# A hybrid encoder: splitting the mixer's weights ahead of the mixer and keeping the parts in DRAM

## The chip, the cores and the metric

One core of a Trainium2 chip runs the whole program. The metric is the device time of one execution in microseconds (us). Five engines take part: PE multiplies matrices (its weight loads are listed apart, as PEld), DVE and POOL work element by element on vectors, ACT evaluates functions and copies, and SP only issues DMAs. Each engine works through its own list of instructions in order; semaphores hold an instruction until what it needs is there.

## The reference

Two layers, on 512 tokens of width 1024, all in float32:

```python
for layer in range(DEPTH):            # DEPTH = 2
    x = x + 0.5 * swiglu(rms_norm(x, ffn1_norm), ffn1_w_in, ffn1_w_out)     # inner width 2816
    x = x + hybrid_mixer(rms_norm(x, mix_norm), w_in, ..., w_out, slopes)
    x = x + 0.5 * swiglu(rms_norm(x, ffn2_norm), ffn2_w_in, ffn2_w_out)

def hybrid_mixer(h, ...):
    aq, ak, av, bu, cq, ck, cv, dq, dk, dv = split(h @ w_in)    # 18 blocks of 128 columns
    o_a = windowed attention with a sink;  o_c = dilated attention;  o_d = neighbourhood attention
    y_b = s5_bidirectional(bu, ...); g = gelu(y_b); y_b = g * sigmoid(g @ w_glu)
    return concat(o_a, y_b, o_c, o_d) @ w_out
```

`s5_bidirectional` is a linear recurrence over the tokens in both directions.

## The kernel before

The activations `x` stay on the chip, transposed: 8 tiles of 128 features by 512 tokens. A product is made at float32 precision from three matmuls (`mm3`, lines 107 to 109): each operand is split into a high part, which is its rounding to the format fp32r, and a low part, the remainder; line 107 multiplies one low part, line 108 the other, line 109 the two high parts. So every weight goes through three steps. `load` (line 113) has SP fetch up to 128x1024 raw weights into a `wr` tile (ring of 2). Then, in pieces of at most 512 columns, line 125 has ACT cast a piece into `wh` (ring of 4), and line 126 subtracts: `wl = wr - wh` (ring of 4). Line 126 runs on DVE, or on POOL where `pooled=True`, which all weights of the mixer have but its first two blocks and `wg`.

`ffn` runs 22 passes over f in four groups. A pass takes two weight tiles of 1024 columns (gate and up), 48 matmuls of 512 columns, and a chain of DVE and ACT operations that writes `a`. After each group, eight products with `w2` (768 or 640 columns) add into `x`. In the first feed-forward of a layer `s5_tables` prepares tables for the recurrence: a Python generator (`hooks`) of which one step is taken per pass, at a lower priority.

`mixer` projects (`wm`, 18 blocks of 1024 columns), does the attentions and the recurrence (`s5`), and merges (`woD`, `woB`, `woC`, `woA`). A string, ORDER, sets the order in which the code calls these steps. In the recurrence DVE scans (lines 823, 825), then `zr` and `zi` are formed from products of DVE (832, 835) and POOL (833, 836, tile `rot`), added on DVE (834, 837), and PE multiplies them (848, 849, into `pyp`). Between these, POOL scales the attention's `p` (694), and DVE subtracts for `pT` (716) and computes a reciprocal root (lines 140 to 145, on 128x16 `rn` and `rq`).

The final order on each engine is chosen by a scheduler that goes by priorities and an estimate of the times; tiles with one tag share a ring, and an instruction that takes a tile waits until its last user is done. The tag `t2` has 15 tiles of 128x512 and serves the feed-forward's `sg` and `af`, the norm's sums, the attention's `p` and others.

Of the kernel before, what the change touches and what calls it, by code (L numbers as in the profile page):

```python
# [11 lines left out]
F32 = mybir.dt.float32  # L12
F32R = mybir.dt.float32r
I32 = mybir.dt.int32
AF = mybir.ActivationFunctionType
ALU = mybir.AluOpType
# [4 lines left out]
P = 128  # L21
S = 512
# [4 lines left out]
DEPTH = 2  # L27
# [6 lines left out]
HOOK = 300  # L34
# [6 lines left out]
T2 = 15  # L41
# [29 lines left out]
def hybrid_encoder(ctx: ExitStack, tc: tile.TileContext, t: dict):  # L71
    nc = tc.nc
    pool = ctx.enter_context(tc.tile_pool(name="sb", bufs=1))
    ps = ctx.enter_context(tc.tile_pool(name="ps", bufs=1, space=PSUM))
    dr = ctx.enter_context(tc.tile_pool(name="dr", bufs=2, space=DRAM))
    tt = nc.vector.tensor_tensor
# [6 lines left out]
    def nm(s):  # L83
        uid[0] += 1
        return f"{s}{uid[0]}"

    def t2(name="t"):
        return pool.tile([P, S], F32, tag="t2", bufs=T2, name=nm(name))

    def k4(shape, dt=F32, name="k"):  # L90
        return pool.tile(shape, dt, tag="k4", bufs=K4, name=nm(name))
# [1 line left out]
    def s8(shape, dt=F32, name="s"):  # L93
        return pool.tile(shape, dt, tag="s8", bufs=S8, name=nm(name))
# [4 lines left out]
    def bank(tag, name=None):  # L99
        bufs = {"mm": 3, "ot": 1, "sc": 2, "tp": 2}[tag]  # L100
        return ps.tile([P, 512], F32, tag=tag, bufs=bufs, name=nm("p" + (name or tag)))

    def f32(ap):
        return ap.bitcast(F32)

    def mm3(out, lh, ll, rh, rl, start, stop):
        nc.tensor.matmul(out, ll, rh, start=start, stop=False)  # L107
        nc.tensor.matmul(out, lh, rl, start=False, stop=False)  # L108
        nc.tensor.matmul(out, lh, rh, start=False, stop=stop)  # L109

    def load(src, cols):
        raw = pool.tile([P, 1024], F32, tag="wr", bufs=2, name=nm("wr"))
        nc.sync.dma_start(raw[:, :cols], src)
        return raw

    def weights(src, cols, step=512, raw=None, pooled=False):
        if raw is None:
            raw = load(src, cols)
        parts = []
        for i in range(0, cols, step):  # L120
            w = min(step, cols - i)
            hi = pool.tile([P, 512], F32R, tag="wh", bufs=4, name=nm("wh"))
            lo = pool.tile([P, 512], F32R, tag="wl", bufs=4, name=nm("wl"))
            r = raw[:, i:i + w]
            nc.scalar.copy(hi[:, :w], r)  # L125
            (nc.gpsimd if pooled else nc.vector).tensor_tensor(lo[:, :w], r, f32(hi[:, :w]), op=ALU.subtract)  # L126
            parts.append((hi, lo))

        def at(c0, n=P):
            hi, lo = parts[c0 // step]  # L130
            o = c0 % step
            return hi[:, o:o + n], lo[:, o:o + n]

        return at
# [352 lines left out]

    def mixer(l, T, next_norm):
        h = state["h"]
        wm = t["wm"]  # L490

        pend = []
        for j in range(2):
            w = weights(wm[l, j], 1024)
            pt = bank("mm", name="pt")
            pend.append((pt, w))
        for j in range(2):
            pt, w = pend[j]
            for k in range(KC - 1):
                mm3(pt, *w(k * P), h[k][0], h[k][1], k == 0, False)  # L500
        for j in range(2):
            pt, w = pend[j]
# [15 lines left out]
        def toks(ap, b):  # L518
            return ap[:, b * P:(b + 1) * P]

        def project(blk0):
            st = {}

            def run(i, k2):
                def go(w):
                    if k2 == 0:
                        st["w"] = w
                    else:
                        w = st["w"]
                    if i == 0 and k2 == 0:  # L530
                        st["pts"] = [bank("mm", name="pr") for _ in range(2)]
                    pts = st["pts"]
                    outs = [pts[b // 2][:, (b % 2) * 256:(b % 2) * 256 + 256] for b in range(4)]
                    for b in range(4):
                        for kk in range(2 * k2, 2 * k2 + 2):
                            k = i * 4 + kk
                            mm3(outs[b], toks(h[k][0], b), toks(h[k][1], b), *w(kk * 256, 256),
                                k == 0 and b % 2 == 0, k == KC - 1 and b % 2 == 1)
                return go

            return st, [(lambda: weights(wm[l, blk0], 1024, pooled=True), run(0, 0)), (None, run(0, 1)),
                        (lambda: weights(wm[l, blk0 + 1], 1024, pooled=True), run(1, 0)), (None, run(1, 1))]

        def then(step, fn):
            ld, run = step
# [76 lines left out]
        def v_perm(blk0, res):  # L622
            vt = []

            st = {}

            def start(w):
                st["w"] = w
                st["pt"] = bank("mm", name="pt")
                for k in range(KC // 2):  # L630
                    mm3(st["pt"], *w(k * P), h[k][0], h[k][1], k == 0, False)

            def run(_):
                pt, w = st["pt"], st["w"]
                for k in range(KC // 2, KC):
                    mm3(pt, *w(k * P), h[k][0], h[k][1], False, k == KC - 1)
                a = t2(name="a")
                nc.scalar.copy(a, pt)
                b = t2(name="vb")
                tt(b.rearrange("p (b r c) -> p r b c", r=8, b=4), a.rearrange("p (r b c) -> p r b c", r=8, b=4),  # L640
                    R.rearrange("p (r b c) -> p r b c", r=8, b=4), op=ALU.mult)
                vt.append(b)

            def flip(_):
                v = s8([P, 4, 4, P], F32R, name="v")
                res.append(v)
                for b2 in range(2):
                    tp = bank("tp", name="tp")
                    for b in range(2):
                        for j in range(2):  # L650
                            c0 = (2 * b + j) * P
                            nc.tensor.transpose(tp[:, c0:c0 + P], vt[j][:, (2 * b2 + b) * P:(2 * b2 + b + 1) * P], ident)
                    src = tp.rearrange("p (b h d) -> p (b h) d", b=2, d=64)
                    dst = v[:, 2 * b2:2 * b2 + 2].rearrange("p b h e -> p (b h) e")
                    nc.scalar.copy(dst[:, :, 0:64], src)
                    tt(dst[:, :, 64:128], src, f32(dst[:, :, 0:64]), op=ALU.subtract)

            load_ = lambda j: lambda: weights(wm[l, blk0 + j], 1024, pooled=True)
            return [(load_(0), start), (None, run), (load_(1), start), (None, run), (None, flip)]

        def attention(res, qk, vs, band, biases, perm, is_a):
# [80 lines left out]
        def merge(name, mt, nk, norm=None):  # L742
            per = {1: 8, 2: 4, 3: 2}[nk]

            st = {}
            half = per // 2

            def run(dd, part):
                def go(w):
                    if part == 0:  # L750
                        st["w"] = w
                    else:
                        w = st["w"]
                    for dj in range(part * half, part * half + half):
                        op = bank("mm", name="op")
                        for i in range(nk):
                            mm3(op, *w((nk * dj + i) * P), mt[i][:, 0], mt[i][:, 1], i == 0, i == nk - 1)
                        d = per * dd + dj
                        tt(x[d], op, x[d], op=ALU.add)
                        if norm is not None:  # L760
                            norm_chunk(norm, d)
                            norm_square(d)
                return go

            steps = []
            for dd in range(KC // per):
                steps.append((lambda dd=dd: weights(t[name][l, dd], nk * per * P, 384 if nk == 3 else 512,
                                                    pooled=True), run(dd, 0)))
                steps.append((None, run(dd, 1)))
            return steps  # L770

# [28 lines left out]
        def s5():  # L800
            zr, zi = k4([P, G, NCH], name="zr"), k4([P, G, NCH], name="zi")
            for half in range(2):
# [6 lines left out]
                a, b = t2("rot"), t2("rot")  # L809
# [19 lines left out]
            for half in range(2):  # L829
                gs = slice(8 * half, 8 * half + 8)  # L830
                a, b = t2("rot"), t2("rot")
# [9 lines left out]
            for half in range(2):  # L841
                gs = slice(8 * half, 8 * half + 8)
                yp = bank("sc", name="yp")
                for i in range(8):
                    g = 8 * half + i
                    o = yp[:, i * 64:(i + 1) * 64]
# [3 lines left out]
                a = t2(name="ga")  # L850
# [7 lines left out]
                yield  # L858
            for j in range(L):
                nc.sync.dma_start(yd.rearrange("g c j n -> j c g n")[j], ys[16 * j:16 * j + 16])  # L860
            gw = weights(t["wg"][l], 512)
            g2 = []
            gs_ = []
            for j in range(2):
# [41 lines left out]
        for token in tokens:  # L906
            if token in streams and token != "s5":
                i = taken.get(token, 0)
# [16 lines left out]
        for i, token in enumerate(tokens):  # L925
# [6 lines left out]
            else:  # L932
                n = taken.get(token, 0)
                taken[token] = n + 1
                stages[token[0]][token[1] == "t"](n // 2, n % 2)
        for _ in streams["s5"]:
            raise AssertionError

    for l in range(DEPTH):
        T = {}  # L940
        hooks = s5_tables(l, T)
        ffn(l, 1, 3 * l + 1, hooks)
        with tc.high_priority(offset=-HOOK):
            for _ in hooks:
                pass
        mixer(l, T, 3 * l + 2)
        ffn(l, 2, 3 * l + 3 if l + 1 < DEPTH else None, None)


def _tables():  # L950
# [108 lines left out]
```

## Time and profile before

| | us |
|---|---|
| median of 3 runs | 2025.49 (2025.34 to 2025.53) |
| the profiled execution | 2025.69 |
| its span, first to last instruction | 2023.9 |
| first feed-forward of layer 0 | 0 to 392 |
| mixer of layer 0 | 392 to 649 |
| second feed-forward of layer 0 | 649 to 1009 |
| layer 1: the same three | 1009, 1396, 1653 to the end |

Times in the profile count from the span's start. The mean granted clock of PE is 0.989 of full speed. An engine's busy time is what it spent in instructions; a PE that is busy all the time can still be one that runs at the lower clock. DMA traffic averages 93 GB/s over the span.

### The profile page before, as it was taken

To read this page: it belongs to the slowest core of one execution; us is meant where nothing else is said; L and a number is where in the kernel's file an instruction comes from. 1 tells how busy PE (TensorE), PEld (TensorE's weight loads), DVE (VectorE), ACT (ScalarE), POOL (GpSimd) and SP (SyncE) were. 2 spreads that over 40 slices of the span, in tenths; PEclk is the share of its full clock that TensorE was granted. 3 is DMA by queue.
4 is the path that set the end of the run, shared out by engine and by line. 5 is a ranking of instruction groups with operands and counts; after the bars stand their busy time and mean duration, and the time that the engine had idled before them with its cause. 6 is when DMAs were issued, how large, how long until landed. Compare 5 with 4: busy or idle time off the path is not lost.

```text
span 2023.9 us, 26161 instructions
## 1 busy us (share of the span) xinstructions
PE 1969.1 (97%) x9768; PEld 1648.9 (81%) x9768; DVE 1240.6 (61%) x2327; ACT 804.4 (40%) x1523; POOL 368.4 (18%) x349
## 2 busy tenths in 40 slices
PE   8999999998999999999999999999989989999999
PEld 6788878897977788888888888888978778888887
DVE  6865547657887545444577655465687875444454
ACT  4333323444676323233442333334547653232332
POOL 4010100254445000000120101002544540000000
PEclk9999999998999999999999999999989999999999
DMA  5232343331312332323233332423313122333233
GB/s 176 82 104 88 104 83 106 97 114 51 97 55 72 97 101 91 97 89 109 84 116 88 102 93 93 102 88 103 119 39 99 50 66 94 99 96 103 81 107 104
DMA packets 74447, 189.24 MB, mean 93 GB/s; under 512 B 16960, under 2 KB 22848, under 8 KB 74320
## 3 DMA queue, kind: packets, MB, share of 16 engines
q1 hardware_dynamic: 74224, 187.51, 30.7%
q8 instruction: 76, 1.25, 0.3%
q14 instruction: 51, 0.42, 0.1%
q0 software_dynamic: 96, 0.07, 0.0%
HBM read 182.86 MB, written 4.69 MB: 93 GB/s over the span
## 4 chain that ended last, share of the span: by engine, by line
PE 83%; DVE 10%; ACT 4%; issue 2%; POOL 1%; DMA 0%; SPq 0%; DVEq 0%; ACTq 0%; POOLq 0%
PE pop L109 9%; PE pop L108 9%; PE pop L107 9%; PE pup L107 7%; PE pgp L107 7%; PE pgp L108 7%; PE pgp L109 7%; PE pup L109 7%; PE pup L108 7%; PE ppr L107 1%; PE ppr L108 1%; PE ppr L109 1%; DVE wl L126 1%; PE pfp L448 1%; DVE hl L186 1%
## 5 line engine op out<-in xcount | busy, mean ns | idle before, releaser
L125 ACT CAST wh<-wr 128x512 fp32r<-128x512 f32 (+2 forms) x718 | 405.9, 570 | 962.8 <-PE pgp L109 314.0
L126 DVE TENSOR_TENSOR wl<-wr,wh 128x512 fp32r<-128x512 f32 (+2 forms) x618 | 409.4, 665 | 380.0 <-ACT wh L125 378.3
L107 PE MATMUL pgp<-hh,wl 128*128 128x512 f32 x704 | 275.5, 391 | 7.6 <-DVE wl L126 7.6
L107 PE MATMUL pup<-hh,wl 128*128 128x512 f32 x704 | 276.3, 392 | 3.2 <-DVE wl L126 3.2
L107 PE MATMUL pop<-a,wl 128*128 128x512 f32 x704 | 277.0, 395 | 1.4 <-DVE wl L126 1.4
L108 PE MATMUL pgp<-hl,wh 128*128 128x512 f32 x704 | 275.5, 391 | 2.4 <-DVE hl L186 2.4
L109 PE MATMUL pop<-a,wh 128*128 128x512 f32 x704 | 276.3, 392 | 0.0
L108 PE MATMUL pop<-a,wh 128*128 128x512 f32 x704 | 274.5, 390 | 0.6 <-DVE a L257 0.6
L108 PE MATMUL pup<-hl,wh 128*128 128x512 f32 x704 | 275.0, 391 | 0.0
L109 PE MATMUL pup<-hh,wh 128*128 128x512 f32 x704 | 275.0, 391 | 0.0
L109 PE MATMUL pgp<-hh,wh 128*128 128x512 f32 x704 | 274.7, 390 | 0.0
L196 POOL TENSOR_TENSOR t<-t,sq 128x512 f32<-128x512 f32 x42 | 60.0, 1430 | 664.9 <-ACT sq L195 663.6
L107 PEld LDWEIGHTS pgp<-hh,wl 128*128 128x128 f32 x704 | 132.6, 188 | 35.7 <-DVE wl L126 8.0
L126 POOL TENSOR_TENSOR wl<-wr,wh 128x512 fp32r<-128x512 f32 (+1 forms) x100 | 131.2, 1317 | 161.7 <-ACT wh L125 125.4
L107 PEld LDWEIGHTS pup<-hh,wl 128*128 128x128 f32 x704 | 132.5, 188 | 33.6 <-DVE wl L126 5.6
L108 PEld LDWEIGHTS pgp<-hl,wh 128*128 128x128 f32 x704 | 132.6, 188 | 32.9 <-DVE hl L186 5.5
L109 PEld LDWEIGHTS pop<-a,wh 128*128 128x128 f32 x704 | 132.2, 188 | 30.6
L108 PEld LDWEIGHTS pop<-a,wh 128*128 128x128 f32 x704 | 132.2, 188 | 30.2 <-DVE a L257 1.0
L107 PEld LDWEIGHTS pop<-a,wl 128*128 128x128 f32 x704 | 132.3, 188 | 28.9 <-DVE wl L126 2.1
L109 PEld LDWEIGHTS pup<-hh,wh 128*128 128x128 f32 x704 | 132.4, 188 | 27.6
L109 PEld LDWEIGHTS pgp<-hh,wh 128*128 128x128 f32 x704 | 132.4, 188 | 27.6
L108 PEld LDWEIGHTS pup<-hl,wh 128*128 128x128 f32 x704 | 132.5, 188 | 27.4
(263 smaller groups left out, 3071.3 us busy)
## 6 DMA issues: line engine op xcount, KB each, us to landing
wr<-in_f_w SPq DMA_DIRECT2D x176, 512.0 KB, 3.4
wr<-in_f_w SPq DMA_DIRECT2D x64, 384.0 KB, 3.1
wr<-in_f_w SPq DMA_DIRECT2D x64, 320.0 KB, 2.9
wr<-in_wm SPq DMA_DIRECT2D x36, 512.0 KB, 3.5
bias<-in_ctab SPq DMA_DIRECT2D x8, 448.0 KB, 3.4
bias<-in_rbx SPq DMA_DIRECT2D x8, 448.0 KB, 3.8
wr<-in_woC SPq DMA_DIRECT2D x8, 384.0 KB, 3.1
x<-in_xt SPq DMA_DIRECT2D x8, 256.0 KB, 6.4
```

The source lines that it names most:

```text
L107: nc.tensor.matmul(out, ll, rh, start=start, stop=False)
L108: nc.tensor.matmul(out, lh, rl, start=False, stop=False)
L109: nc.tensor.matmul(out, lh, rh, start=False, stop=stop)
L125: nc.scalar.copy(hi[:, :w], r)
L126: (nc.gpsimd if pooled else nc.vector).tensor_tensor(lo[:, :w], r, f32(hi[:, :w]), op=ALU.subtract)
L186: stt(hl, x[c], gcol, f32(hh), op0=ALU.mult, op1=ALU.subtract)
L196: gtt(acc, acc, sq, op=ALU.add)
L448: nc.tensor.matmul(pt[r0:r0 + 64, c0 + 16:c0 + 144], bm[q][:, g].rearrange("p a c -> p (a c)"), v[q][:, g].rearrange("p j c -> p (j c)"), ...
```

## The change

A new generator, `presplit(l)`, goes through all weights of the mixer of layer `l` in 55 pieces. For each piece SP loads it (`praw`), ACT casts (`phi`), DVE subtracts (`plo`), all three in tiles of the ring `t2`, and POOL's queue stores both parts in DRAM tiles. For layer 0 three pieces are made per pass of its first feed-forward, beside a step of `s5_tables`; for layer 1 three per pass of the second feed-forward of layer 0. The mixer's calls of `weights(...)` become `stored(...)`, which has SP load both parts into `wh` and `wl`. No `wr` tile is used in the mixer any more, and POOL splits nothing.

```diff
-    def t2(name="t"):
-        return pool.tile([P, S], F32, tag="t2", bufs=T2, name=nm(name))
+    def t2(name="t", dt=F32):
+        return pool.tile([P, S], dt, tag="t2", bufs=T2, name=nm(name))
...
-            (nc.gpsimd if pooled else nc.vector).tensor_tensor(lo[:, :w], r, f32(hi[:, :w]), op=ALU.subtract)
+            tt(lo[:, :w], r, f32(hi[:, :w]), op=ALU.subtract)
...
+    kept = {}
+
+    def presplit(l):
+        wo = lambda n, per: [(n, i, t[n][l, i], per * P) for i in range(t[n].shape[1])]
+        todo = [("wm", j, t["wm"][l, j], 1024) for j in range(18)]
+        todo += wo("woD", 8) + wo("woC", 6) + wo("woB", 8) + wo("woA", 8) + [("wg", 0, t["wg"][l], 512)]
+        for name, j, src, cols in todo:
+            step = 384 if name == "woC" else 512
+            for i in range(0, cols, step):
+                raw, hi, lo = t2(name="praw"), t2(name="phi", dt=F32R), t2(name="plo", dt=F32R)
+                nc.sync.dma_start(raw[:, :step], src[:, i:i + step])
+                nc.scalar.copy(hi[:, :step], raw[:, :step])
+                tt(lo[:, :step], raw[:, :step], f32(hi[:, :step]), op=ALU.subtract)
+                dst = [dr.tile([P, step], F32, name=nm("pd")) for _ in range(2)]
+                nc.gpsimd.dma_start(dst[0], f32(hi[:, :step]))
+                nc.gpsimd.dma_start(dst[1], f32(lo[:, :step]))
+                kept.setdefault((l, name, j), []).append(dst)
+                yield
+
+    def stored(l, name, j):
...
+        for dst in kept.pop((l, name, j)):
+            hi = pool.tile([P, 512], F32R, tag="wh", bufs=4, name=nm("wh"))
+            lo = pool.tile([P, 512], F32R, tag="wl", bufs=4, name=nm("wl"))
+            nc.sync.dma_start(f32(hi[:, :step]), dst[0])
+            nc.sync.dma_start(f32(lo[:, :step]), dst[1])
             parts.append((hi, lo))
...
-            load_ = lambda j: lambda: weights(wm[l, blk0 + j], 1024, pooled=True)
+            load_ = lambda j: lambda: stored(l, "wm", blk0 + j)
...
+    def both(a, b, n):
+        live = True
+        while live:
+            live = next(a, 0) is None
+            for _ in range(n):
+                live |= next(b, 0) is None
+            yield
+
     for l in range(DEPTH):
         T = {}
         hooks = s5_tables(l, T)
+        if l == 0:
+            hooks = both(hooks, presplit(0), 3)
         ffn(l, 1, 3 * l + 1, hooks)
...
-        ffn(l, 2, 3 * l + 3 if l + 1 < DEPTH else None, None)
+        later = both(iter(()), presplit(l + 1), 3) if l + 1 < DEPTH else iter(())
+        ffn(l, 2, 3 * l + 3 if l + 1 < DEPTH else None, later)
+        with tc.high_priority(offset=-HOOK):
+            for _ in later:
+                pass
```

The scheduler's order moves with it. On POOL, in the recurrence of the first mixer, before (`wl` of line 126 are splits, `rot` of 833 and 836 the products for `zr` and `zi`, `p` the attention's scaling):

```order
L833 TENSOR_TENSOR rot_4232<-si_4115,k_2624 128x512
L126 TENSOR_TENSOR wl_4201<-wr_4198,wh_4200 128x512
L694 TENSOR_SCALAR p_4054<-p_4054,ll_4050 128x256
L694 TENSOR_SCALAR p_4060<-p_4060,ll_4050 128x384
L694 TENSOR_SCALAR p_4081<-p_4081,ll_4050 128x384
L694 TENSOR_SCALAR p_4087<-p_4087,ll_4050 128x256
L126 TENSOR_TENSOR wl_4205<-wr_4198,wh_4204 128x512
L126 TENSOR_TENSOR wl_4415<-wr_4412,wh_4414 128x512
L836 TENSOR_TENSOR rot_4233<-sr_4114,k_2624 128x512
L126 TENSOR_TENSOR wl_4419<-wr_4412,wh_4418 128x512
L833 TENSOR_TENSOR rot_4262<-si_4115,k_2624 128x512
```

The same place on POOL now (833 is 866 there, 836 is 869, 694 is 728):

```order
L866 TENSOR_TENSOR rot_4756<-si_4641,k_3134 128x512
L728 TENSOR_SCALAR p_4580<-p_4580,ll_4576 128x256
L728 TENSOR_SCALAR p_4586<-p_4586,ll_4576 128x384
L728 TENSOR_SCALAR p_4607<-p_4607,ll_4576 128x384
L728 TENSOR_SCALAR p_4613<-p_4613,ll_4576 128x256
L869 TENSOR_TENSOR rot_4757<-sr_4640,k_3134 128x512
L866 TENSOR_TENSOR rot_4786<-si_4641,k_3134 128x512
```

The four splits are gone; the products and the scalings keep their order. On DVE, before, the small operations of lines 140 to 145 stand ahead of the sum `zi` of line 837:

```order
L834 TENSOR_TENSOR zr_3639<-zr_3639,rot_4232 128x512
L716 TENSOR_TENSOR pT_4193<-ptp_4190,pT_4193 128x256
L573 TENSOR_TENSOR ss_4146<-ss_4146,ec_3350 128x16
L716 TENSOR_TENSOR pT_4244<-ptp_4240,pT_4244 128x384
L140 TENSOR_SCALAR rn_4158<-ss_4146 128x16
L141 TENSOR_SCALAR rn_4158<-rn_4158 128x16
...
L143 TENSOR_TENSOR rq_4159<-rn_4158 128x16
L144 SCALAR_TENSOR_TENSOR rq_4159<-rq_4159,ss_4146 128x16
L837 TENSOR_TENSOR zi_3640<-zi_3640,rot_4233 128x512
L145 SCALAR_TENSOR_TENSOR rn_4158<-rq_4159,rn_4158 128x16
```

On DVE now (837 is 870, 140 is 176):

```order
L867 TENSOR_TENSOR zr_4175<-zr_4175,rot_4756 128x512
L750 TENSOR_TENSOR pT_4768<-ptp_4764,pT_4768 128x384
L607 TENSOR_TENSOR ss_4672<-ss_4672,ec_3896 128x16
L870 TENSOR_TENSOR zi_4176<-zi_4176,rot_4757 128x512
L750 TENSOR_TENSOR pT_4777<-ptp_4773,pT_4777 128x384
L176 TENSOR_SCALAR rn_4684<-ss_4672 128x16
```

`zi` has moved ahead of that chain. On SP, near the end of the first mixer, now (`pd` are the stored parts; 384 columns mark `woC`):

```order
L162 DMA wl_6350<-pd_2562 128x384
L161 DMA wh_6349<-pd_2561 128x384
L810 DMA bias_6163<-in_atab 128x384
L810 DMA bias_14411<-in_ctab 128x896
L810 DMA bias_14715<-in_ctab 128x896
L162 DMA wl_6354<-pd_2572 128x384
L162 DMA wl_6374<-pd_2582 128x384
L162 DMA wl_6378<-pd_2697 128x384
L161 DMA wh_6353<-pd_2571 128x384
L161 DMA wh_6373<-pd_2581 128x384
L161 DMA wh_6377<-pd_2696 128x384
```

Before, two loads of raw `woC` tiles stood there; now three loads of low parts stand ahead of the high part that belongs to the first of them.

## Rows read from the trace of the kernel before

**Rows 1.** The page, part 1: busy time, share and instructions of each engine.

```profile
PE 1969.1 (97%) x9768; PEld 1648.9 (81%) x9768; DVE 1240.6 (61%) x2327; ACT 804.4 (40%) x1523; POOL 368.4 (18%) x349
```

**Rows 2.** Windows: us, busy by engine (instructions), granted clock, DMA share, GB/s.

```profile
0.00:392.00 392.00, 382.85 (x1755) 312.22 (x1756) 248.02 (x487) 137.72 (x244) 50.78 (x38) 1.00 0.36 105
392.00:649.00 257.00, 239.04 (x1529) 214.19 (x1528) 188.59 (x401) 145.49 (x312) 123.42 (x133) 0.95 0.27 83
649.00:1009.00 360.00, 357.41 (x1571) 293.23 (x1570) 185.46 (x282) 124.03 (x216) 15.81 (x11) 1.00 0.30 92
111.00:177.00 66.00, 66.00 (x295) 54.54 (x294) 43.11 (x57) 22.47 (x37) 7.96 (x3) 1.00 0.30 92
```

**Rows 3.** Waits of PE, whole span: us in total, times, longest.

```profile
PE pyp L849 <- DVE zi L837: 11.3, 2, 5.7
PE ppr L108 <- POOL wl L126: 0.7, 2, 0.4
```

**Rows 4.** Timeline of PE, gaps in the mixer: start, us; idle before, releaser.

```profile
469.84 0.44 PE L677 MATMUL psc<-o,o 128*128 128x384 f32 x1 [1.18 <-DVE mn L680]
...
491.90 0.69 PE L849 MATMUL pyp<-zi,s 128*128 128x64 f32 x2 [5.67 <-DVE zi L837]
...
588.62 0.97 PE L107 MATMUL pop<-mt,wl 128*128 128x512 f32 x3 [1.62 <-ACT mt L885]
...
623.40 0.97 PE L107 MATMUL pop<-mt,wl 128*128 128x512 f32 x3 [1.82 <-ACT mt L736]
```

**Rows 5.** Windows of low granted clock, columns as in rows 2.

```profile
488.40:505.50 17.10, 13.60 (x64) 13.53 (x65) 9.91 (x23) 5.65 (x10) 1.77 (x2) 0.50 0.10 31
...
624.90:628.30 3.40, 3.40 (x12) 2.85 (x11) 2.00 (x4) 1.98 (x4) 0.97 (x2) 0.51 0.00 0
1495.30:1508.90 13.60, 13.09 (x61) 13.02 (x62) 6.94 (x15) 5.61 (x10) 0.00 (x0) 0.50 0.00 1
```

**Rows 6.** Timeline of POOL in the recurrence of the first mixer.

```profile
476.17 1.74 POOL L126 TENSOR_TENSOR wl<-wr,wh 128x512 fp32r<-128x512 f32 x1
479.32 3.01 POOL L694 TENSOR_SCALAR p<-p,ll 128x256 f32<-128x256 f32 x4 [1.41 <-DVE ll L690]
482.29 2.95 POOL L126 TENSOR_TENSOR wl<-wr,wh 128x512 fp32r<-128x512 f32 x2
485.21 1.30 POOL L836 TENSOR_TENSOR rot<-sr,k 128x512 f32<-128x512 f32 x1
```

**Rows 7.** Timeline of DVE in the same stretch.

```profile
463.64 0.69 DVE L656 TENSOR_TENSOR v<-ptp,v 128x512 fp32r<-128x512 f32 x1 [2.06 <-ACT v L655]
...
485.31 1.23 DVE L141 TENSOR_SCALAR rn<-rn 128x16 int32<-128x16 int32 x1
...
490.24 0.17 DVE L143 TENSOR_TENSOR rq<-rn 128x16 f32<-128x16 f32 x1
...
491.16 0.68 DVE L837 TENSOR_TENSOR zi<-zi,rot 128x512 f32<-128x512 f32 x1
```

**Rows 8.** The page, part 5: busy us, mean ns of one, idle before.

```profile
L125 ACT CAST wh<-wr 128x512 fp32r<-128x512 f32 (+2 forms) x718 | 405.9, 570 | 962.8 <-PE pgp L109 314.0
L126 DVE TENSOR_TENSOR wl<-wr,wh 128x512 fp32r<-128x512 f32 (+2 forms) x618 | 409.4, 665 | 380.0 <-ACT wh L125 378.3
...
L126 POOL TENSOR_TENSOR wl<-wr,wh 128x512 fp32r<-128x512 f32 (+1 forms) x100 | 131.2, 1317 | 161.7 <-ACT wh L125 125.4
```

**Rows 9.** DMA issues: KB each, us to landing; last, POOL's timeline.

```profile
wr<-in_f_w SPq DMA_DIRECT2D x176, 512.0 KB, 3.4
...
ud<-us SPq DMA_DIRECT2D x4, 256.0 KB, 2.3
...
wr<-in_wg SPq DMA_DIRECT2D x2, 256.0 KB, 2.7
...
dmask<-in_dmask POOLq DMA_DIRECT2D x1, 56.0 KB, 5.8
...
2.60 0.54 POOL L171 DMA_DIRECT2D dmask<-in_dmask  x1
```

More of the change, by code (lines that the diff above doesn't have):

```diff
@@ L114, in load, with weights @@
         return raw
-    def weights(src, cols, step=512, raw=None, pooled=False):
+    def weights(src, cols, step=512, raw=None):
         if raw is None:
@@ L125, in weights, with at @@
             nc.scalar.copy(hi[:, :w], r)
-            (nc.gpsimd if pooled else nc.vector).tensor_tensor(lo[:, :w], r, f32(hi[:, :w]), op=ALU.subtract)
+            tt(lo[:, :w], r, f32(hi[:, :w]), op=ALU.subtract)
+            parts.append((hi, lo))
+        def at(c0, n=P):
+            hi, lo = parts[c0 // step]
+            o = c0 % step
+            return hi[:, o:o + n], lo[:, o:o + n]
+        return at
+    kept = {}
[16 more added lines that the diff above has]
+    def stored(l, name, j):
+        step = 384 if name == "woC" else 512
+        parts = []
+        for dst in kept.pop((l, name, j)):
[3 more added lines that the diff above has]
+            nc.sync.dma_start(f32(lo[:, :step]), dst[1])
             parts.append((hi, lo))
@@ L489, in mixer @@
         h = state["h"]
-        wm = t["wm"]
         pend = []
         for j in range(2):
-            w = weights(wm[l, j], 1024)
+            w = stored(l, "wm", j)
             pt = bank("mm", name="pt")
@@ L539, in run @@
                 return go
-            return st, [(lambda: weights(wm[l, blk0], 1024, pooled=True), run(0, 0)), (None, run(0, 1)),
-                        (lambda: weights(wm[l, blk0 + 1], 1024, pooled=True), run(1, 0)), (None, run(1, 1))]
+            return st, [(lambda: stored(l, "wm", blk0), run(0, 0)), (None, run(0, 1)),
+                        (lambda: stored(l, "wm", blk0 + 1), run(1, 0)), (None, run(1, 1))]
         def then(step, fn):
@@ L766, in merge @@
             for dd in range(KC // per):
-                steps.append((lambda dd=dd: weights(t[name][l, dd], nk * per * P, 384 if nk == 3 else 512,
-                                                    pooled=True), run(dd, 0)))
+                steps.append((lambda dd=dd: stored(l, name, dd), run(dd, 0)))
                 steps.append((None, run(dd, 1)))
@@ L860, in s5 @@
                 nc.sync.dma_start(yd.rearrange("g c j n -> j c g n")[j], ys[16 * j:16 * j + 16])
-            gw = weights(t["wg"][l], 512)
+            gw = stored(l, "wg", 0)
             g2 = []
```

## The prediction

> **What bounds the kernel now.** I read the engine table first: PE is busy 1969.1 of 2023.9 us, 97% [rows 1]. So a saved ACT, DVE or POOL instruction is worth nothing by itself; only time in which PE stands still, or runs slowly, can be won. The stage windows say where that is. The first feed-forward (0 to 392) has PE busy 382.85 of 392 us, the second (649 to 1009) 357.41 of 360. A stretch in the middle of a feed-forward, 111 to 177, which holds six passes over f, shows no PE idle at all. The mixer (392 to 649) has 239.04 of 257: 18 us idle, and a granted clock of 0.95 [rows 2]. The second layer repeats this 1004 us later, so what is said of one mixer counts twice.
>
> The waits name it. Few of PE's mixer waits end on what this change removes: POOL's split ends PE's wait only 0.7 us in all. The largest wait is for `zi` of line 837, 11.3 us in two waits [rows 3], one per mixer: PE idles 5.67 us in front of the first `pyp` matmul on `zi` [rows 4]. And the clock of 0.95 is no even loss: 17.1 us from 488.4 and 13.6 us from 1495.3 ran at 0.50, the lower level of 1.2 GHz, and both begin inside or at the end of that wait [rows 5]. Shorter gaps differ: after 1.18 us idle PE went on at the full clock, after 1.82 us it fell to 0.51 for 3.4 us [rows 4, 5].
>
> Why is `zi` late? POOL in that stretch: a `wl` split of 1.74 us, four scalings of `p`, two more splits in 2.95 us, and only then the product `rot` that `zi` needs, without a gap from 479.3 on [rows 6]. DVE in the same stretch: a 128x16 `rn` takes 1.23 us at 485.31, while POOL runs, and its sister 0.17 us at 490.24, when POOL is done; `zi` stands behind eleven such small operations and starts at 491.16 [rows 7]. So a DVE instruction waits for the POOL instruction that is running. The Trainium skill says the same (SBUF — State Buffer, section Who interferes with whom): a DVE instruction with two SBUF inputs is blocked for the whole of a POOL instruction that reads SBUF. The two durations agree.
>
> **The change, part by part.** The profiled execution took 2025.69 us (span 2023.9 and 1.8 around it), the median of the runs is 2025.49; I sum against the first.
>
> *Removed from each mixer.* 55 casts on ACT at 570 ns, 50 splits on POOL at 1317 ns (131.2 us for 100), 5 on DVE at 665 ns [rows 8], and 28 loads of the raw weights. By itself nothing, since PE waits for none of them. But the splits in rows 6 go, 1.74 and 2.95 us of POOL ahead of `rot`. In the new order nothing but four `p` scalings (3.01 us in the trace) stands between the products on POOL, and DVE's `zi` stands ahead of the chain of small operations instead of inside it. DVE had waited 2.06 us for ACT just before the scans that start the chain, so it was not late at 463.6 [rows 7]. POOL then ends `rot` near 483.6 (479.3 + 3.0 + 1.3), and `zi` follows at 484 to 485. PE stood ready at 486.2 (491.9 less 5.67), or up to 1.2 us earlier if the gap of 1.18 us ahead goes too. I take 0.7 us of wait left of 5.67: 5.0 us won per mixer, 10.0 in all. The bounds are 0 (the order does not help) and 5.7.
>
> *The clock.* If PE no longer stands still for longer than 1.2 us there, the stretches at 0.50 do not come: half of 17.1 and of 13.6 us, 15.4 us in all. The bounds are 0 and 15.4. I take the whole, since the residual 0.7 us is below the 1.18 us after which the clock stayed up.
>
> *Other waits in the mixer.* The gap of 1.62 us at 588.6 waits for ACT, where a cast of `wh` stands directly ahead; I take half, 0.8 us, twice: 1.6 us. The gap of 1.82 us at 623.4 waits for a cast at the end of attention without any split before it, so it stays, with its drop of the clock.
>
> *Added to each mixer: the loads.* 110 loads of 256 KB (192 KB for `woC`) for 55 raw pieces, 13.9 MB more; 83 GB/s over 257 us becomes 137. At 92 GB/s the share of the engines was 0.30 [rows 2], so about 0.45. A 256 KB load lands 2.7 us after its issue [rows 9]; the split it replaces took 0.6 + 1.3 us after the buffer came free. The ring of four holds three pieces ahead, and the fastest pieces last 2.1 us (nine matmuls at 66 us for 288 [rows 2]), so 6 us of cover. Two places have less. At the mixer's start the first pair of loads stands on SP behind two 512 KB loads for the next feed-forward: I take 1 us per mixer. At the end, three `wl` loads stand on SP ahead of `wh` of the first of them, and the last two wait until PE has let go of `woC` pieces that the third `mt` holds; three such loads then need some 3.9 us (2.7 and two more transfers at the 307 GB/s that 92 GB/s at a share of 0.30 imply), of which I take 1.5 us per mixer as not covered by the matmuls in between. That is 5 us in all; bounds 0 and 16 (a 2.7 us load, not hidden, three times per mixer).
>
> *Added to two feed-forwards (both of layer 0).* Per feed-forward 55 loads, 55 casts, 55 subtractions on DVE and 110 stores on POOL's queue. ACT gets 31 us and has 255 free. DVE gets 37 us on 248 of 392 and 185 of 360: free time is there, and PE's weights are split four pieces, some 8 us, ahead, so a late DVE is felt only beyond that. POOL's issue of a 128-row DMA took 0.54 us [rows 9]: 59 us, on a POOL that is busy 51 and 16 us. By the rows the cost of that issue to DVE is between 0 and 59 us of blocked DVE per feed-forward, and even then DVE reaches 344 of 392. I take 0, the trace having only one such issue, with no DVE instruction beside it.
>
> The Trainium skill (SBUF — State Buffer, section Who interferes with whom) says, as an inference, that descriptor generation needs the write side of the shared pair and a tensor_tensor takes only the read side, which would make it 0. It also warns (SBUF — State Buffer, section SBUF: two separate sides) that DVE operations in a two-port mode hold POOL's descriptors back, so that stores come late; no run here shows either yet, and the sum goes by neither.
>
> The traffic: 41.7 MB more per feed-forward, 211 and 208 GB/s instead of 105 and 92, a share near 0.7. PE uses a 512 KB block in 5.5 us (66 us for twelve); its load has about 9 us, and takes 3.4. SP carries the `praw` loads in one line with these, and each of them waits for a `t2` buffer that a store must release. I take 1 us lost per feed-forward, 2 us in all; the upper bound is the second rival.
>
> Sum: 10.0 + 15.4 + 1.6 - 5 - 2 = 20 us: 2025.69 - 20 = 2005.7, and 0.2 less against the median: **2005.5 us**. Its own range is 1994 to 2016.
>
> **The rivals.** *The wait moves instead of going.* `zi` comes only 2.5 us earlier, or a late `wh` takes its place, PE still stands more than 1.6 us near there, and the clock falls as before: 2 x 2.5 + 1.6 - 7 = 0, so 2025, between 2016 and 2029. For it: DVE's other work there (scans, `pT`) stays, and new waits on loads come in. Against: the three splits were 4.7 us of POOL in just this stretch.
>
> *The feed-forward becomes slower (the other side).* Place: SP, where `praw` waits for a store. Of 15 `t2` buffers about nine are free for three pieces of three tiles. Three pieces come per f, each f is 11 us, or 16.5 with the second product's share. A piece lives 2.7 + 0.57 + 0.67 + 2 x 0.54 us and the landing of its store: 7.3 us with the 2.3 us of a 256 KB store from SP, 10.8 with the 5.8 us of the only DMA of comparable row count on POOL's queue [rows 9]. It decides from a landing of about 6 us (11 us per f) to 11 us (16.5). Above it, the loads of PE's weights stand behind `praw`. At 1.2 us too much, 19 groups, two feed-forwards: 46 us, so 2052.
>
> The Trainium skill names this side as well (DMA: Bandwidth & Descriptors, section Issuing engines are not separate DMA queues): a second issuing queue brings no second set of DMA engines. The trace has too little on POOL's queue to test it.
>
> *More than forecast.* DVE, no longer blocked by 50 POOL splits per mixer, also shortens half of the 12 us of other idle per mixer: 12 us more, 1993, down to 1986.
>
> **How the numbers follow.** Forecast 0.55, moved wait 0.20, slower feed-forward 0.16, more 0.09. A measurement of this kernel tells about 0.2% from nothing, 4 us: same is 2021.4 to 2029.5. The moved wait gives 0.08 to faster, 0.10 to same and 0.02 to slower: faster 0.72, same 0.10, slower 0.18. The range 1990 to 2033 leaves out some 0.06 below and 0.12 above.
>
> **What would show it.** Right: the wait for `zi` under 1.5 us, no stretch of 0.50 clock longer than 4 us in either mixer, small DVE operations near 0.17 us there, and PE without idle in the feed-forwards of layer 0. Wrong: PE waits on `wl` or `wh` loads in the mixer above 3 us each; SP waits on stores, and PE idle in the feed-forwards of layer 0 while those of layer 1 stay as they were; stores landing later than 6 us.

## The result, and the profile after

The changed kernel takes 2074.36 us (median of 2073.39 to 2076.61), the kernel before 2025.41 beside it: ratio 1.0243, 95% interval 1.0226 to 1.0261. It is slower by 49 us where 20 us of gain were forecast, and outside the range. The profiled span is 2072.7 us.

Windows cut at the starts of the stages tell where the time went. Their columns are those of [rows 2]. First the kernel before: first feed-forward of layer 0, mixer, second feed-forward of layer 0 together with the first of layer 1, mixer of layer 1, last feed-forward.

```profile
0.00:392.20 392.20, 383.05 (x1756) 312.39 (x1757) 248.22 (x487) 137.81 (x245) 50.78 (x38) 1.00 0.35 105
392.20:648.20 256.00, 238.04 (x1524) 213.38 (x1524) 187.59 (x399) 144.60 (x310) 123.42 (x133) 0.95 0.27 82
648.20:1396.10 747.90, 744.42 (x3362) 610.31 (x3362) 431.03 (x762) 256.39 (x452) 58.39 (x37) 1.00 0.32 96
1396.10:1651.80 255.70, 237.79 (x1524) 213.11 (x1524) 189.53 (x399) 144.61 (x310) 123.95 (x133) 0.96 0.25 78
1651.80:2023.80 372.00, 365.81 (x1607) 299.73 (x1605) 184.23 (x284) 120.96 (x210) 11.87 (x8) 1.00 0.31 96
```

The same five stages of the changed kernel:

```profile
0.00:438.10 438.10, 390.87 (x1756) 316.30 (x1757) 281.62 (x543) 166.48 (x301) 113.69 (x149) 0.96 0.58 190
438.10:682.20 244.10, 232.59 (x1523) 210.36 (x1524) 167.04 (x393) 114.98 (x254) 56.98 (x82) 0.97 0.45 141
682.20:1455.30 773.10, 753.91 (x3363) 615.73 (x3361) 460.84 (x817) 281.82 (x506) 118.86 (x148) 0.99 0.46 147
1455.30:1699.80 244.50, 233.94 (x1523) 212.64 (x1524) 167.24 (x394) 116.20 (x255) 57.25 (x83) 0.97 0.44 137
1699.80:2072.60 372.80, 365.77 (x1606) 299.99 (x1604) 184.16 (x284) 120.89 (x210) 11.91 (x8) 1.00 0.31 95
```

The mixers got shorter, by 11.9 and 11.2 us, 23.1 in all. The two feed-forward stages that split ahead got longer, by 45.9 and 25.2 us, 71.1 in all. The last one, where nothing is split ahead, moved by 0.8. In the two longer stages PE's idle time (stage less PE busy) went from 9.15 to 47.23 and from 3.48 to 19.19 us, 53.8 more; the other 17 us are PE working longer at a lower clock (0.96 and 0.99 for 1.00).

PE's waits name what it waited for; the `zi` row answers to the first of [rows 3], and is down from 11.3 us to 2.2:

```profile
PE pup L107 <- DVE sg L286: 33.9, 7, 11.0
PE pop L107 <- DVE sg L286: 13.4, 4, 7.7
...
PE pyp L882 <- DVE zi L870: 2.2, 2, 1.1
```

`sg` is the DVE instruction that reads the first product out of its PSUM bank. There are three `mm` banks, so the `up` product of one f needs the bank of the `gp` product of the f before, and gets it when `sg` of that f is done. In the kernel before no wait for `sg` is among PE's waits of the first feed-forward. One of the two longest now stands near the end of this stage (timeline; in brackets the idle time before and its releaser), on PE, DVE, ACT and SP in turn:

```profile
378.77 0.79 PE L107 MATMUL pup<-hh,wl 128*128 128x512 f32 x1 [8.83 <-DVE sg L286]
```

```profile
371.35 0.69 DVE L515 TENSOR_SCALAR k<-k 64x1024 f32<-64x1024 f32 x1
372.07 1.29 DVE L148 TENSOR_TENSOR plo<-praw,phi 128x512 fp32r<-128x512 f32 x2
377.42 0.69 DVE L148 TENSOR_TENSOR plo<-praw,phi 128x512 fp32r<-128x512 f32 x1 [4.06 <-ACT phi L147]
378.03 0.68 DVE L286 TENSOR_TENSOR sg<-pgp,R 128x512 f32<-128x512 f32 x1
```

```profile
371.36 1.25 ACT L147 CAST phi<-praw 128x512 fp32r<-128x512 f32 x2 [0.77 <-DMA praw<-in_woB]
376.77 0.62 ACT L147 CAST phi<-praw 128x512 fp32r<-128x512 f32 x1 [4.16 <-DMA praw<-in_woA]
```

```profile
367.57 0.42 SPq L146 DMA_DIRECT2D praw<-in_woA  x1
371.34 0.33 SPq L113 DMA_DIRECT2D wr<-in_f_w  x1
371.71 0.43 SPq L146 DMA_DIRECT2D praw<-in_woA  x1
```

Read it from the bottom. SP issues `praw` at 371.71, directly behind a `wr` load that had to wait for its ring. The piece lands some 5 us later. ACT's cast waits 4.16 us for it, DVE's subtraction 4.06 us for the cast, and `sg` stands behind the subtraction, though PE had ended its product near 359, as PE's timeline shows:

```profile
358.67 0.39 PE L109 MATMUL pgp<-hh,wh 128*128 128x512 f32 x1
358.90 0.39 PE L107 MATMUL pup<-hh,wl 128*128 128x512 f32 x1
```

DVE's line was late even before that, with the table work (`k`) ahead of the pieces. PE wants the bank at 369.94 (378.77 less 8.83), has none and stands 8.83 us.

The longest wait is of another make:

```profile
61.91 0.80 PE L107 MATMUL pup<-hh,wl 128*128 128x512 f32 x1 [10.98 <-DVE sg L286]
```

In these 10.98 us DVE stood idle for `phi` only 1.05 us; some 6 us went to table steps of the recurrence that stand ahead of `sg` in its list, and 1.8 us to subtractions of pieces. Of the 37.0 us that PE waited for `sg` in the first stage, DVE stood idle for `phi` in 11.3, did table steps in 9.0 and subtracted pieces in 6.9. So two things stand in front of `sg` there: pieces that wait for a load, and plain work. The other four waits for `sg`, 10.3 us, lie between 733 and 877, where layer 0's second feed-forward has no table steps. At the longest, 5.38 us at 733.61, DVE had stood idle for `phi` in 6.5 of the last 16 us.

Over the whole kernel ACT's casts and DVE's subtractions waited (busy, mean ns, idle before):

```profile
L147 ACT CAST phi<-praw 128x512 fp32r<-128x512 f32 (+1 forms) x110 | 66.4, 604 | 133.5 <-DMA praw<-in_wm 82.5 <-DMA praw<-in_woC 25.7 <-DMA praw<-in_woD 11.1
L148 DVE TENSOR_TENSOR plo<-praw,phi 128x512 fp32r<-128x512 f32 (+1 forms) x110 | 73.6, 670 | 113.8 <-ACT phi L147 113.6
```

And the landings (KB each, median us), which answer to [rows 9]:

```profile
wr<-in_f_w SPq DMA_DIRECT2D x176, 512.0 KB, 3.5
...
pd<-phi POOLq DMA_DIRECT2D x94, 256.0 KB, 3.5
pd<-plo POOLq DMA_DIRECT2D x94, 256.0 KB, 4.3
wl<-pd SPq DMA_DIRECT2D x94, 256.0 KB, 2.8
...
praw<-in_wm SPq DMA_DIRECT2D x72, 256.0 KB, 5.1
```

PE's own weights land as before (3.5 against 3.4), the stores below 6 us. Only `praw` is late, 5.1 where I had counted 2.7.

### The profile page after: what moved, and what is told of

Its sections match the earlier page's. It is cut to its first block, busy times and chain, and to the rows that moved or that the text cites. A ratio compares the mean times of both kernels' runs of the same rounds, so it can differ in the third digit from the quotient of the medians.

```text
span 2072.7 us, 27307 instructions
## 1 busy us (share of the span) xinstructions
PE 1977.1 (95%) x9768; PEld 1655.0 (80%) x9768; DVE 1260.9 (61%) x2427; ACT 800.4 (39%) x1523; POOL 358.7 (17%) x469
## 5 line engine op out<-in xcount | busy, mean ns | idle before, releaser
L125 ACT CAST wh<-wr 128x512 fp32r<-128x512 f32 (+1 forms) x608 | 338.2, 563 | 732.6 <-PE pgp L109 232.6
L126 DVE TENSOR_TENSOR wl<-wr,wh 128x512 fp32r<-128x512 f32 (+1 forms) x608 | 405.8, 671 | 318.2 <-ACT wh L125 316.9
L107 PE MATMUL pup<-hh,wl 128*128 128x512 f32 x704 | 281.2, 399 | 36.6 <-DVE sg L286 33.9
L108 PEld LDWEIGHTS pop<-a,wh 128*128 128x128 f32 x704 | 133.5, 190 | 29.1
L148 DVE TENSOR_TENSOR plo<-praw,phi 128x512 fp32r<-128x512 f32 (+1 forms) x110 | 73.6, 670 | 113.8 <-ACT phi L147 113.6
L150 POOL DMA_DIRECT2D pd<-phi x110 | 59.8, 544 | 476.8 <-ACT phi L147 457.5
## 6 DMA issues: line engine op xcount, KB each, us to landing
pd<-phi POOLq DMA_DIRECT2D x94, 256.0 KB, 3.5
pd<-plo POOLq DMA_DIRECT2D x94, 256.0 KB, 4.3
wl<-pd SPq DMA_DIRECT2D x94, 256.0 KB, 2.8
wh<-pd SPq DMA_DIRECT2D x94, 256.0 KB, 3.0
praw<-in_wm SPq DMA_DIRECT2D x72, 256.0 KB, 5.1
```

The costliest lines, as they stand in the source:

```text
L126: tt(lo[:, :w], r, f32(hi[:, :w]), op=ALU.subtract)
L148: tt(lo[:, :step], raw[:, :step], f32(hi[:, :step]), op=ALU.subtract)
L150: nc.gpsimd.dma_start(dst[0], f32(hi[:, :step]))
```

## The experiments

The theory: instructions for a late load stand in ACT's and DVE's lines in front of the feed-forward's own `sg`, and PE waits for its bank. The rivals: the traffic as such, the stores, or the added work as such. Each ratio is against the kernel before on the same chip. "Stages" are the two that lost, 392.2 and 747.9 us before, 438.1 and 773.1 after, cut in the same way.

**The halves apart.** Without the pieces; the mixer loads parts from DRAM tiles filled once:

```diff
-                raw, hi, lo = t2(name="praw"), t2(name="phi", dt=F32R), t2(name="plo", dt=F32R)
...
+                kept.setdefault((l, name, j), []).append([d[:, :step] for d in few[len(kept) % 2]])
```

> The mixer's half of the change alone: no pieces are split ahead in the feed-forwards of layer 0; the mixer loads its high and low parts from four DRAM tiles that are written once at the start (so the parts are not those of its weights; the traffic of the loads is that of the change). The mixers of the changed kernel were 11.8 and 11.3 us shorter by their stages. If the feed-forwards alone carry the loss, this kernel takes 2025.4 - 23 = 2002 us (1998 to 2008). If part of the mixers' gain had come from a feed-forward that left more loaded ahead, it is above 2012.

Measured 2002.04 us, ratio 0.9886 [0.9859, 0.9913]; stages 392.2 and 748.7. The other half, with the pieces made and stored but the mixer splitting its own weights:

```diff
-            nc.sync.dma_start(f32(hi[:, :step]), dst[0])
-            nc.sync.dma_start(f32(lo[:, :step]), dst[1])
+            nc.scalar.copy(hi[:, :step], r)
+            split(lo[:, :step], r, f32(hi[:, :step]), op=ALU.subtract)
```

> The feed-forwards' half alone: the pieces are loaded, split and stored in front of the mixer as in the change, but nobody reads them; the mixer splits its weights itself, as before. By the stage starts of the two traces (first feed-forward +45.9, second +26 to 29) it takes 2025.4 + 72 = 2097 us (2088 to 2106). If the feed-forward's loss had come from the mixers' loads that run ahead into it, it is below 2080.

Measured 2092.5 us, 1.0336 [1.0321, 1.0352]. Both within what was written: the halves nearly add up (-22.3 and +68.1 us, 45.8 for 49), the mixer's is a gain of 1.1%, the feed-forwards' a loss of 3.4%.

**Without the stores.**

```diff
-                nc.gpsimd.dma_start(dst[0], f32(hi[:, :step]))
-                nc.gpsimd.dma_start(dst[1], f32(lo[:, :step]))
```

> The change without its 220 stores: the pieces are loaded, cast and subtracted as in the change, and thrown away; the mixer loads its parts from four DRAM tiles written once. Theory (a cast and a subtraction wait on ACT and DVE for a late praw load, and the feed-forward's own sg stands behind them): the loads and the waits stay, so most of the 72 us stays, 2055 to 2076 us. Rival (the stores: their traffic, their issue on POOL, or the t2 buffers they hold): 2002 to 2025 us.

Measured 2049.29 us, 1.0122 [1.0107, 1.0137], just below the theory's span. The stages are 435.5 and 756.3: the first keeps 43.3 of its 45.9 us, the second only 8.4 of 25.2. So the stores are no cause of their own in the first, but help to cause the second. The `praw` row shows how they could: it lands in 3.8 us without them, 5.1 with them. DVE's waits for `phi` go the same way as the losses: from 43.7 to 36.7 us in the first stage, from 69.9 to 39.6 in the second.

```profile
praw<-in_wm SPq DMA_DIRECT2D x72, 256.0 KB, 3.8
```

**Without the praw loads** (the cast and the subtraction read an on-chip constant):

```diff
-                nc.sync.dma_start(raw[:, :step], src[:, i:i + step])
-                nc.scalar.copy(hi[:, :step], raw[:, :step])
+                rawb = bc(ident, 1, step // P)
+                nc.scalar.copy(v(hi), rawb)
```

> The change without its 110 praw loads: the cast and the subtraction read a constant on-chip tile (the identity, repeated) instead, with the same shapes; stores and mixer loads as in the change. Theory (late praw loads): the loss in the feed-forwards goes, 2002 to 2015 us. Rival (the added work itself: 31 us of ACT, 37 of DVE and 59 of POOL's issue per feed-forward, or the stores): 2055 to 2075 us.

Measured 2017.85 us, 0.9957 [0.9940, 0.9973], 3 us above the theory's span. The stages lose 13.3 and 0.6 us instead of 45.9 and 25.2, although casts, subtractions and stores are all there. The added work as such costs at most these 13.9 of the 71.1 us and is not the main cause.

**The traffic alone**: all loads and stores, but no cast and no subtraction.

```diff
-                nc.scalar.copy(hi[:, :step], raw[:, :step])
-                tt(lo[:, :step], raw[:, :step], f32(hi[:, :step]), op=ALU.subtract)
...
+                nc.gpsimd.dma_start(dst[0], raw[:, :step])
```

> All loads and stores of the change, but no cast and no subtraction of the pieces: both stores take the raw piece, so the parts that the mixer loads are not high and low parts. Theory (the loss is instructions that wait in ACT's and DVE's lines for praw): the traffic alone costs the feed-forwards 0 to 10 us over the mixer's half alone (2002), 2002 to 2012 us. Rival (the traffic, or SP and POOL held by it): 2040 to 2075 us.

Measured 2013.01 us, 0.9940 [0.9928, 0.9953], 1 us above the theory's span. The same bytes move and the engines see 210 and 152 GB/s; the stages lose 6.6 and 1.2 us:

```profile
0.00:398.80 398.80, 384.26 (x1756) 311.96 (x1756) 249.84 (x487) 139.10 (x246) 109.41 (x149) 1.00 0.62 210
...
646.60:1395.70 749.10, 745.23 (x3362) 610.14 (x3360) 428.81 (x762) 255.85 (x451) 117.69 (x148) 1.00 0.47 152
```

Here too `praw` lands in 5.2 us, but POOL alone waits for it. The traffic by itself falls as a rival. (The run takes one `t2` tile per piece for three, so it says little on that ring.)

**Which engine.** With the cast, without DVE's subtraction:

```diff
-                tt(lo[:, :step], raw[:, :step], f32(hi[:, :step]), op=ALU.subtract)
...
-                nc.gpsimd.dma_start(dst[1], f32(lo[:, :step]))
+                nc.gpsimd.dma_start(dst[1], f32(hi[:, :step]))
```

> The change without the subtractions on DVE (the cast's result is stored twice, so the low parts are wrong); ACT's casts still wait for praw. If PE's loss comes by way of DVE (sg behind plo), most of it goes: 2008 to 2035 us. If a cast that waits on ACT, with silu and the casts of PE's own weights behind it, costs the same by itself: 2050 to 2075 us.

Measured 2034.67 us, 1.0049 [1.0036, 1.0061], just inside the first span; stages 419.4 and 751.8, so +27.2 and +3.9. The subtraction on DVE accounts for 40 of the 71.1 us, 21.3 of 25.2 in the second stage. The cast that waits on ACT, over the traffic alone, costs 20.6 and 2.7: less, but not nothing. PE's waits there, 11.8 us for `sg` and 9.9 for `wl`, fit silu and ACT's casts of PE's weights standing behind the waiting cast; the two were not separated.

**The load ahead of its use.** Every piece stays, on the same engines, but `praw` is written three pieces earlier:

```diff
-                nc.sync.dma_start(raw[:, :step], src[:, i:i + step])
+        fetch(3)
+        for _ in range(3):
+            yield
...
+            fetch(n + 4)
```

> The whole change, but each praw load is written three pieces (one pass over f) ahead of its cast and subtraction. Theory (cast and subtraction wait for a late praw load, sg behind them): most of the loss goes, 2005 to 2030 us, and the wait of phi for praw (about 115 us in the changed kernel's ACT row) falls under 30 us. Rival (the traffic and the added work by themselves): 2060 to 2075 us.

Measured 2022.31 us, 0.9990 [0.9981, 0.9999], 52 us less than the change. The stages are 408.8 and 748.7 (+16.6 and +0.8). The cast's row, PE's wait for `sg` and the load's row decide it:

```profile
L161 ACT CAST phi<-praw 128x512 fp32r<-128x512 f32 (+1 forms) x110 | 63.3, 602 | 5.3 <-DMA pd<-phi 4.5 <-DMA praw<-in_wm 0.5 <-DVE a L307 0.3
```

```profile
PE pup L107 <- DVE sg L300: 2.3, 1, 2.3
```

```profile
praw<-in_wm SPq DMA_DIRECT2D x72, 256.0 KB, 5.1
```

The load is as slow as in the change, 5.1 us, and the traffic the same; but ACT's idle time before the casts falls from 133.5 to 5.3 us, 0.5 of it for the load, and PE's waits for `sg` fall from 47.3 to 2.3 us. So the loss did not come from a slow load, but from users that the program put right behind it.

The run does not separate two ways in which that acts, since the scheduler's order moved with the lead. By 61 us DVE had started two `sg` in the change and four here, and from 30 us on had done 12.1 us of table steps there and 6.3 here. At the end of the stage the two orders are nearly alike, with three pieces ahead of the same `sg`: PE waits 8.83 us in the change, 2.33 here and 2.33 in the run without the loads. Of the difference of 6.5 us some 4.1 are DVE's wait for `phi`, some 2 are two table steps and a split that the change also had ahead of `sg`. In the second feed-forward, without table steps, DVE's 69.9 us of waits for `phi` go, and of the 25.2 us of loss 0.8 are left. How the first stage's loss divides between waiting instructions and their order was not measured; no run holds the order and removes the wait.

The 13 to 17 us that the first stage still loses, here and without the loads, stay open. PE's waits there are for `sg` 2.3 us in both, for `a` 4.6 here and 5.8 without the loads, and here also 4.6 for `wl` splits ahead of the second product.

**The split on POOL.** Cast and subtraction on POOL, without and with the lead:

```diff
-                nc.scalar.copy(hi[:, :step], raw[:, :step])
-                tt(lo[:, :step], raw[:, :step], f32(hi[:, :step]), op=ALU.subtract)
+                nc.gpsimd.tensor_copy(hi[:, :step], raw[:, :step])
+                gtt(lo[:, :step], raw[:, :step], f32(hi[:, :step]), op=ALU.subtract)
```

> The whole change, but the cast and the subtraction of the pieces stand on POOL, so that neither ACT nor DVE waits for praw; all loads and stores stay. Theory (sg and silu stand behind instructions that wait for praw): the loss goes but for what POOL's 110 operations per feed-forward cost DVE beside it, 2002 to 2025 us. Rival (traffic: PE's own weights come late): 2050 to 2075 us. If POOL's operations block DVE for their whole time (some 55 x 2.5 us = 140 us on a DVE with 100 us free), it is above 2075 us.

> Both edits together: praw three pieces ahead on SP, cast and subtraction on POOL. Theory: SP, too, is then not held by a praw load that waits for a buffer, 2000 to 2015 us, not slower than the better of the two alone by over 4 us. If POOL's work blocks DVE it is slower than the lead alone.

Measured 2110.08 us, 1.0433 [1.0395, 1.0470], and 2098.37 us, 1.0370 [1.0352, 1.0388]. My main expectation failed in both, and the case written for a blocked DVE came. In the first stage of the first run DVE has 488 instructions, nearly as the kernel before (487), but is busy 289.69 us instead of 248.22:

```profile
0.00:466.50 466.50, 400.37 (x1756) 321.51 (x1757) 289.69 (x488) 139.32 (x246) 222.87 (x259) 0.94 0.54 179
```

Single ones show it: a split of 0.69 us takes 2.46, a table step of 0.27 takes 1.79 in the same stretch, where POOL's subtractions of 1.3 us run from 49.37 and from 52.27.

```profile
48.82 2.46 DVE L126 TENSOR_TENSOR wl<-wr,wh 128x512 fp32r<-128x512 f32 x1
51.20 0.67 DVE L354 TENSOR_SCALAR sm<-sm 128x112 f32<-128x112 f32 x1
51.90 1.79 DVE L356 TENSOR_TENSOR sm<-sm 128x112 f32<-128x112 f32 x1
```

POOL's work took back on DVE more than the 36.7 us that it freed there. How the rest of the loss divides was not measured apart.

**Praw on POOL's queue.**

```diff
-                nc.sync.dma_start(raw[:, :step], src[:, i:i + step])
+                nc.gpsimd.dma_start(raw[:, :step], src[:, i:i + step])
```

> The whole change, but the praw loads are issued from POOL's queue, not from SP's, where they stand behind loads that wait for PE's ring. If the place in SP's line makes praw late: 2010 to 2040 us. If praw is late because its 256 KB share the transfer engines with the stores and with 512 KB loads (or because on POOL it now stands behind stores that wait for the subtraction): 2055 to 2080 us.

Measured 2205.01 us, 1.0903 [1.0884, 1.0921], far beyond both. `praw` now lands faster (3.6 us), and yet it is the worst of all, because on POOL it stands behind the store of the piece before:

```profile
797.03 0.54 POOL L150 DMA_DIRECT2D pd<-phi  x1 [3.63 <-ACT phi L147]
797.56 0.55 POOL L146 DMA_DIRECT2D praw<-in_wm  x1
...
802.11 0.54 POOL L150 DMA_DIRECT2D pd<-phi  x1 [3.46 <-ACT phi L147]
802.64 0.55 POOL L146 DMA_DIRECT2D praw<-in_wm  x1
```

A chain of 5.08 us per piece: load, cast, store, next load. ACT and DVE run at its pace, and PE's waits for `sg` come to 140.5 us. Moving the load out of SP's line is no substitute for a lead.

**A version that beats both.** First the lead, with layer 1 alone split ahead; then also 14 pieces of layer 0, those whose splits stood on POOL around `zi` [rows 6]:

```diff
+        if l == 0:
+            todo = [w for w in todo if w[0] == "wm" and 8 <= w[1] < 15]
+            for _ in range(5):
+                yield
...
-            hooks = both(hooks, presplit(0), 3)
+            hooks = both(hooks, presplit(0), 1)
```

> The lead of three pieces, and only layer 1's weights are split ahead (in the second feed-forward of layer 0); layer 0's mixer splits its own, as before. With the lead that feed-forward lost under 1 us, and a mixer with stored parts is 11 to 12 us shorter: 2025 - 12 + 1 = 2014 us (2011 to 2018).

> As the run with layer 1 alone, and of layer 0 only the 14 pieces whose splits stood on POOL around zi (blocks 8 to 14 of wm), one piece per f, loaded three ahead, from the sixth f on, when DVE's work on the tables is mostly done. If the first feed-forward loses under 3 us by that and layer 0's mixer gains most of its 12: 2004 to 2010 us, faster than both kernels. If the gain needs all pieces: 2014 us, as with layer 1 alone.

Measured 2014.21 us, 0.9947 [0.9933, 0.9960], as computed, and, with the 14 pieces, 2007.30 us, 0.9906 [0.9891, 0.9920], faster than both kernels. In the second, layer 0's mixer is 238.8 us for 256.0 with only 14 of its 55 pieces stored, and the first feed-forward is 402.9:

```profile
0.00:402.90 402.90, 385.66 (x1756) 313.70 (x1757) 254.23 (x501) 144.57 (x259) 65.54 (x66) 0.99 0.42 129
402.90:641.70 238.80, 228.13 (x1524) 204.97 (x1523) 176.24 (x399) 136.86 (x296) 103.22 (x119) 1.00 0.33 103
```

So in this execution the few splits beside `zi` were enough for the mixer's gain; PE had the full clock there (1.00, 0.95 before), and 9.9 of the 17.2 us are its shorter busy time. The first feed-forward lost 10.7 us, though, where I had written under 3: 5.3 of it is one wait for a `wl` split on DVE. That stage stays the weak point of every version that splits ahead in it.

## Why the prediction was wrong

**The failed step is the feed-forward term.** The prediction put it as "PE's weights are split four pieces, some 8 us, ahead, so a late DVE is felt only beyond that", and took 1 us per feed-forward, 2 in all. The stages lost 71.1 us. DVE does two things for PE: it makes `wl`, with those 8 us of cover, and it empties the banks. I counted the first alone. `sg` has one pass over f, 11 us (from 359 to 369.94 in the rows above), and in the first feed-forward much of that was already spent on table work. Then I added DVE's work as busy time (37 us on a DVE with room for it) and not as instructions that wait in a line. Without the loads the work costs 13.9 us in both stages, and with loads that come in time 17.4. The other 54 to 57 us come from pieces whose load is late, by DVE's waits and by the order of its list; how they divide stays open.

**The landing.** I took 2.7 us for a 256 KB load from [rows 9]; it was 5.1 under the new traffic. The lead of three pieces removes about three quarters of the loss (53.7 of 71.1 us) without making the load faster, so this was not the decisive error. But a load issued together with its user is exposed for its whole time.

**The mixers, right in sum by luck.** The forecast for them adds up to 22.0; measured 23.1. The waits for `zi` fell from 11.3 to 2.2 us, 9.1 of the 10.0. The order on POOL is as read from the listing, four scalings and then `rot`, and `zi` now ends before the chain of small operations, which take 0.17 us:

```profile
533.12 1.85 DVE L870 TENSOR_TENSOR zi<-zi,rot 128x512 f32<-128x512 f32 x1
534.89 0.55 DVE L750 TENSOR_TENSOR pT<-ptp,pT 128x384 fp32r<-128x384 f32 x1
535.36 0.16 DVE L176 TENSOR_SCALAR rn<-ss 128x16 int32<-128x16 int32 x1
535.55 0.17 DVE L177 TENSOR_SCALAR rn<-rn 128x16 int32<-128x16 int32 x1
```

The clock term of 15.4 us was too high; PE's busy time in the mixers fell by 9.3. Half of a stretch counts only where PE is busy, 13.60 and 13.09 us of the two [rows 5], so 13.3 was the most. And while the stretches of 17.1 and 13.6 us are gone, others came. In the second mixer one followed the `zi` wait, although that was 1.10 us, shorter than the 1.18 us on which the prediction relied (PE's timeline, and a window with the columns of [rows 2]):

```profile
1549.47 0.44 PE L882 MATMUL pyp<-zi,s 128*128 128x64 f32 x2 [1.10 <-DVE zi L870]
```

```profile
1551.80:1558.60 6.80, 6.80 (x36) 6.80 (x36) 6.29 (x16) 2.50 (x5) 0.00 (x0) 0.50 0.01 2
```

In the first mixer PE went on at the full clock after 1.12 us. So the length of the gap alone did not decide.

PE's idle time in the mixers fell by 13.8 us, where 6.6 was forecast (10.0 + 1.6 - 5). The wait for `mt` gave 0.3 of its 1.6 us (3.2 to 2.9 in both mixers). The loads cost 3.8 us of the 5; PE's largest wait for one is the last row below. The remaining 8.2 us came from waits that the sum left out, above all for `pT` (the kernel before, then the changed one):

```profile
PE pot L719 <- DVE pT L716: 5.8, 8, 1.2
```

```profile
PE pot L753 <- DVE pT L750: 0.7, 2, 0.4
...
PE ppt L107 <- DMA wl<-pd: 2.2, 2, 1.7
```

A clock term 6.1 us too high met 8.2 us that were not in the sum. And in seven runs whose two mixers load all parts, the change among them, the pair was 17.3 to 31.0 us shorter than before, so agreement to 1 us says little.

**The rivals.** The one that ends on the slower side named the right stages and about two thirds of the price (46 us for 71.1), but another mechanism: stores that land later than 6 us and hold `t2`. They land in 3.5 and 4.3 us, SP's `praw` waited for one of them once, 6.7 us, and the traffic alone costs 7.8 us with all of them. What I wrote there as the sign, PE idle in layer 0's feed-forwards while layer 1's stay, was the right thing to look at; the chance of 0.16 was too low, because I weighed one way only by which a late piece could reach PE. The moved wait did not come. The larger gain did not come as a time, but waits of the kind that it named did shrink, by the 8.2 us above; that DVE's freedom from POOL's splits did it was not tested.

The Trainium skill (PSUM — Partial Sum Buffer, section Engine vs sequencer instructions) says that the queues of ACT, DVE and POOL are strict first-in first-out. The trace agrees: `sg` at 378.03 starts only when `plo` of 377.42 is through, with its input long there.

## What to carry to other kernels

Work that is "free" because an engine has idle time is free only if it never waits there: ask what stands behind each added instruction on its engine, and by when PE needs that (a bank to be emptied counts as much as an operand). Issue a load well ahead of the cast that uses it; with a lead of three pieces the same traffic and the same work cost 17 us instead of 71. Read the new order of each list, too: here plain table steps in front of `sg` were the larger part of the longest wait. And before moving all work of a kind, find the few instructions that delay PE: in one profiled execution 14 of 55 pieces brought layer 0's mixer all of its gain.

## What the runs showed of the hardware

A POOL DMA issue hardly held DVE back: in the run with the traffic alone POOL makes 110 issues of 0.54 us in the first stage, and DVE's 487 instructions are busy 249.84 us there, 248.22 before. POOL's casts and subtractions did hold it, as above. The Trainium skill says both, the first as an inference (SBUF — State Buffer, section Who interferes with whom); here the rows agree. Of the two rows that the prediction compares in [rows 7], the one of 1.23 us has one SBUF input. The pair with two is line 143, 0.17 us at 490.24 there and, beside POOL's subtraction from 486.48 in the same trace:

```profile
486.58 1.18 DVE L143 TENSOR_TENSOR rq<-rn 128x16 f32<-128x16 f32 x1
```

The same mixer code with stored parts took 238 to 251 us in these runs, at a granted clock of 0.95 to 0.99. A difference of a few us between two versions therefore says little unless it is taken by stage. The stage lengths above are one profiled execution each, and that execution lies up to 6 us from its median (1995.74 for 2002.04 us with the mixer's half, 2039.81 for 2034.67 with the cast alone).
